# Queries and keys of a head group projected side by side, 512 columns wide

## The chip, the cores and the metric

The kernel runs on one core of a Trainium2 chip. The metric is the device time of one execution in microseconds (us); a result is the median of several runs. The engines are named as in the profile: PE (TensorE, matrix products), PEld (its loads of stationary operands, which overlap with products), DVE (VectorE), ACT (ScalarE), POOL (GpSimd), and SP, whose queue issues most transfers.

## The reference

A trunk of two layers works on 640 tokens: 512 of a new prompt, and 8 running streams with 16 new tokens each. The residual has 1024 features. Each layer is a mixer and a channel mixer, each behind an RMS norm:

```python
# layer 0: gated spatial mixing beside a short gated convolution, then the channel mixer
# layer 1, the mixer that the change is about (for the prompt):
z = x @ w_in                                  # 1024 -> 3072 + 16
q, k, v, f = jnp.split(z, [D_C, 2 * D_C, 3 * D_C], axis=-1)
q = _rmsnorm(q.reshape(b, t, 16, 64), q_norm) # norm over the 64 of a head
k = _rmsnorm(k.reshape(b, t, 16, 64), k_norm)
logf = jax.nn.log_sigmoid(f + b_f)            # "forget values", one a token and head
d = jnp.cumsum(logf, axis=1)
s = einsum('bthd,bshd->bhts', q, k) * 64 ** -0.5 + d_query - d_key
s = where(k_pos <= q_pos, s, NEG_INF)
o = einsum('bhts,bshd->bthd', softmax(s), v)
y = o.reshape(b, t, 1024) @ w_out
# channel mixer, both layers
z = causal_conv3(x @ w_up); y = (silu(gate) * up) @ w_down
```

The streams do the same, each with 256 cached keys and values ahead of its 16 new ones. Outputs are the 640 rows, the new states of the convolutions, and the new keys (behind their norm), values and forget values. All is float32.

## The kernel before

**Arithmetic.** A large product is made of three products of split operands: `weights()` loads a unit of 128 x 1024 float32 weights through SP's queue into `raw`, ACT casts it to `whi` (L88), and DVE subtracts that from `raw` to give the rest, `wlo` (L89). The activations are split likewise into `hh` and `hl`. A product is then hh x whi, hl x whi and hh x wlo. `raw`, `whi` and `wlo` live in the pool `wts` with three buffers each. Products with `whi` or `wlo` take these split operands; transposes, the value products and the streams' products take plain float32.

**Stages.** First mixer, first channel mixer, projections and attention, output projection, second channel mixer. Everything outside the attention has weights stationary and 320 tokens moving (L109), save the first mixer's values (L239: activations stationary, 512 weight columns moving). Engines execute their queues in order. The order of each queue is set when the program is built, by a scheduler that goes by a timeline of its own; buffers of the pools (their `bufs`) limit how far work can run ahead.

**Projections.** The 16 heads are four groups of four. `project(g, ...)` makes queries, keys and values of a group one after the other: for each kind, two units of weights (4 chunks of the features x 256 columns, `io["w_c"]`), and for each of five blocks of 128 tokens 24 matmuls of 256 columns (L507: 8 chunks x 3 products). Two token blocks share a PSUM bank `pj` of 512 columns, of which there are two. ACT evacuates each block into `z` (L510), squares it (L515), DVE sums the squares by head (L516), the root is made by DVE (L151) and POOL (L152), and DVE scales all five blocks by it at once (L519, 1280 elements a partition), for keys once more by the norm's weights (L521). The buffers:

```python
zt = self.zp.tile([P, 5, 256], F32, tag="qk" if kind < 2 else "v", name=k.nm("z"), bufs=3 if kind < 2 else 2)
```

Queries and keys share three such buffers, values have two.

**Forget values.** `decay` is called once, between queries and keys of group 0: 48 matmuls `pf` (L109), a spread of the norm's root over the tokens (matmuls at L174, through `pt`), the logarithm and the running sums `dh`, `dl`, and transfers of these on SP's queue to scratch in HBM (`s_b`, `s_d`, `s_n`; L455 is the first), from which each group reads its rows back (L552 into `kb`; others into `sl` and `sr`).

**Attention.** For each group: transposes (L537) make stacked operands `qa`, `ka`, `qb`, `kb` of two heads (a pair); a prompt block is 128 queries of one head: scores from two matmuls into `sc` (L569, L570), mask (L571), softmax (maximum L589, exponential on ACT L591, reciprocal L592, scaling L594), transposes of the weights `p` into `pt` (L576), a copy `u` (L579 on DVE or ACT), and the value product into `pv` (L583). A pair of streams: `scs` (L634, L641, L644), softmax, transposes (L655), value products (L662), and a transpose back (L666). Within a head pair, which is half a group's attention, eight prompt blocks and two stream pairs follow in a fixed order:

```python
for st in ("b30", "s0", "b31", "o", "b20", "s1", "b21", "b10", "b11", "b00", "b01"):
```

The results are `o[0]` to `o[7]`, two a group. PSUM has two banks for `pj`, two for `sc`, three for `pt`, one for `pv`.

**Filler.** PE needs other work while DVE and ACT do a softmax. This is the next group's projections, and for group 3 the part of the output projection that needs the first three groups only, `po` (L109, also in the `pj` banks):

```python
cut = [6, 6, 6, 6, 6, 4, 4, 4]
for ob in (6, 7, 0, 1, 2, 3, 4, 5):
```

Output blocks 6, 7 and 5 go over four chunks `o[0]` to `o[3]` there, the others over six; the two of group 2 are `o[4]` and `o[5]`. What is left of the output projection comes as blocks `mm` behind the attention.

Of the kernel before, what the change touches and what calls it, by code (L numbers as in the profile page):

```python
# [8 lines left out]
F32 = mybir.dt.float32  # L9
# [34 lines left out]
# columns of the constants of the attention  # L44
# [4 lines left out]
NS = 256 + 16      # keys of a stream  # L49


class Core:
    def __init__(self, ctx, tc, io):
# [38 lines left out]
    def split(self, pool, tags, src):  # L92
        """float32 [128, 640] -> (hi, lo) float32r tiles"""
# [7 lines left out]
    # ---- products, weights stationary, tokens moving  # L101
# [13 lines left out]
    def blocks(self, units, acts, order=None):  # L115
        """one output block for each unit; all share the walk over k, the last chunk closes"""
# [8 lines left out]
    # ---- RMS norm: operands scaled by g now, by the root later  # L125
# [28 lines left out]
    def stats(self, acc, pool, aux):  # L154
        """1/rms for each token, as columns [128, 5]"""
# [8 lines left out]
    def spread(self, rt, pool, aux):  # L164
        """columns [128, 5] -> the same along the free axis of every partition"""
# [45 lines left out]
    # ---- the first mixer  # L211
    def mixer_ab(self, x, load, stats, ring, finish):
        nc, io = self.nc, self.io
        rpool, rtags = ring
        with ExitStack() as es:
            mp = self.pool(es, "ab", bufs=1)
            so = mp.tile([P, 4 * 18], F32, name="sob")
            # v, tokens on partitions
# [24 lines left out]
            # the mask: a query in the first half of a chunk sees no key of the second half  # L243
# [17 lines left out]
            for j in range(4):  # L261
                # gated causal convolution
# [19 lines left out]
            for g in range(4):  # L282
                # spatial gating
# [20 lines left out]
    def project(self, w, acts, order, x, finish, cols=1024, out=None):  # L304
        """x += w^T acts, the first two blocks side by side"""
# [10 lines left out]
    def last_block(self, w, acts, x, out):  # L316
        """the block that ends the program: one half of the tokens leaves while the other is at work"""
# [13 lines left out]
    # ---- the channel mixer  # L331
# [43 lines left out]
class Attention:  # L375
    """forgetting attention of 16 heads: 512 prompt tokens, and 8 streams of 16 behind 256 cached ones"""

    def __init__(self, k, es, rt, o):
# [10 lines left out]
        # sums of the streams as a product over 18 rows: the queries' sums (two parts) against ones,  # L389
        # selectors of (stream, head) against minus the keys' sums (two parts)  # L390
# [22 lines left out]
    def decay(self, h, es):  # L413
        """log forget values and their running sums, heads on partitions"""
# [12 lines left out]
        # log sigmoid(y) = min(y, 0) - log1p(e), e = exp(-|y|)  # L427
# [10 lines left out]
        # running sums, from zero at the start of each stream  # L438
# [25 lines left out]
        # minus the keys' sums, (stream, head) on partitions: cached, then new  # L464
# [12 lines left out]
        # selector rows, the same for each pair of streams  # L477
# [4 lines left out]
        nc.sync.dma_start(out=f(self.sl[2:18]), in_=f(sr))  # L482

    def project(self, g, h, first, after_q=None):
        """q, k, v of four heads, tokens on partitions"""
        k, nc, io = self.k, self.nc, self.io
        z = []
        for kind in range(3):
            if kind == 1 and after_q is not None:
                after_q()  # L490
# [402 lines left out]
```

## Time and profile before

| | |
|---|---|
| median of three runs | 1533.6 us (1533.28 to 1536.43) |
| profiled execution | span 1531.9 us, the only time that the profile gives for it; the median lies 1.7 us above |
| PE, PEld | busy 1517.8 us (99%), 1473.5 us (96%) |
| DVE, ACT, POOL | 59%, 37%, 15% |
| TensorE clock granted | full in all 40 slices of the span |
| HBM | 125.41 MB read, 11.54 MB written: 89 GB/s over the span |
| start of the projections | 679.6 us |
| first attention scores | 738.95 us |
| `po` | from 965.5, to 1030.6 us |
| rest of the output projection from | 1039.1 us |

How to read rows of the trace: a group's row gives line, engine, operation, output <- inputs by the program's names, then partitions x elements, the number of instructions, the busy time in us and the mean of one in ns, and after a second bar the idle time of that engine ahead of them with what ended it. A row of the timeline begins with the start and the duration in us. A row by stretch gives its start and end, its length and the busy time of each engine, with the instructions in brackets. Busy times of PE overlap a little from one instruction to the next, so that the spacing of starts, and not the duration of one, tells what it costs.

### The profile page before, as it was taken

The page shows a single profiled execution, that of the slowest core. Times are in us where ns is not written, and L with a number is a line of the kernel's source. Part 1 is how long each engine was busy: PE and PEld are TensorE (multiplying, and loading weights), DVE is VectorE, ACT ScalarE, POOL GpSimd, SP SyncE. Part 2 cuts the span into 40 slices and gives each one's busy share as a digit, 9 for nine tenths or more (in the row PEclk, how much of TensorE's full clock was granted, in tenths as well). Part 3 has the DMA queues.
Part 4 walks back from the last instruction along what each step waited for, and adds up shares of the span by engine and source line. Part 5 has one row for each costly group of instructions (what it writes and reads, how often), then busy time and mean ns, then how long its engine had stood idle before and what let it go on. Part 6 is the DMA issues. An engine that isn't in the chain of part 4 may idle for free.

```text
span 1531.9 us, 26648 instructions
## 1 busy us (share of the span) xinstructions
PE 1517.8 (99%) x11008; PEld 1473.5 (96%) x11008; DVE 899.1 (59%) x1541; ACT 559.4 (37%) x918; POOL 237.4 (15%) x281
## 2 busy tenths in 40 slices
PE   8999999999999999999999999999999999999999
PEld 6999999999999999999989888888999999999998
DVE  6545437644653655675676766768765466365463
ACT  5422334322322322345545454535432233133231
POOL 5000122201210201143111111003221021021010
PEclk9999999999999999999999999999999999999999
DMA  6222212222223222243544343523222222321313
GB/s 226 77 82 73 77 56 85 68 81 85 62 64 95 64 66 93 62 156 103 180 128 136 122 123 104 183 60 107 83 60 76 87 67 57 98 73 53 107 47 106
DMA packets 52296, 142.90 MB, mean 93 GB/s; under 512 B 6656, under 2 KB 13744, under 8 KB 52048
## 3 DMA queue, kind: packets, MB, share of 16 engines
q1 hardware_dynamic: 45424, 133.79, 28.6%
q10 hardware_dynamic: 6752, 7.41, 1.4%
q8 instruction: 87, 1.43, 0.4%
q14 instruction: 33, 0.27, 0.1%
HBM read 125.41 MB, written 11.54 MB: 89 GB/s over the span
## 4 chain that ended last, share of the span: by engine, by line
PE 96%; DVE 2%; issue 1%; ACT 1%; DMA 0%; POOL 0%; SPq 0%; DVEq 0%; ACTq 0%
PE mm L109 71%; PE pj L507 10%; PE pv L583 3%; PE po L109 2%; PE pt L576 1%; PE mm L239 1%; PE pt L662 1%; PE sc L569 1%; DVE hl L132 1%; PE sc L570 1%; DVE wlo L89 1%; PE scs L641 1%; PE pt L537 1%; PE pt L655 0%; PE scs L634 0%
## 5 line engine op out<-in xcount | busy, mean ns | idle before, releaser
L88 ACT CAST whi<-raw 128x1024 fp32r<-128x1024 f32 (+4 forms) x222 | 207.6, 937 | 494.6 <-PE mm L109 426.1
L109 PE MATMUL mm<-hl,whi 128*128 128x320 f32 x1664 | 379.4, 309 | 0.5 <-DVE hl L132 0.5
L109 PE MATMUL mm<-hh,whi 128*128 128x320 f32 x1664 | 379.8, 309 | 0.0
L109 PE MATMUL mm<-hh,wlo 128*128 128x320 f32 x1664 | 379.2, 309 | 0.0
L109 PEld LDWEIGHTS mm<-hl,whi 128*128 128x128 f32 x1664 | 278.2, 188 | 0.7 <-DVE hl L132 0.7
L109 PEld LDWEIGHTS mm<-hh,whi 128*128 128x128 f32 x1664 | 278.2, 188 | 0.1
L109 PEld LDWEIGHTS mm<-hh,wlo 128*128 128x128 f32 x1664 | 278.0, 188 | 0.0
L89 DVE TENSOR_TENSOR wlo<-raw,whi 128x1024 fp32r<-128x1024 f32 (+4 forms) x222 | 245.5, 1107 | 33.3 <-ACT whi L88 33.0
L109 PE MATMUL mm<-sh,wlo 128*128 128x320 f32 x866 | 197.2, 309 | 1.3 <-DVE wlo L89 1.3
L109 PE MATMUL mm<-sl,whi 128*128 128x320 f32 x866 | 197.2, 309 | 0.0
L109 PE MATMUL mm<-sh,whi 128*128 128x320 f32 x866 | 196.2, 309 | 0.0
L202 POOL COPY so<-zp 128x18 f32<-128x18 f32 x88 | 89.4, 1016 | 570.4 <-DVE zp L191 570.4
L190 DVE TENSOR_TENSOR zp<-mm,rb 128x512 f32<-128x512 f32 x88 | 60.9, 692 | 195.8 <-PE mm L109 195.8
L209 DVE TENSOR_TENSOR x<-mm,x 128x640 f32<-128x640 f32 x79 | 65.0, 823 | 185.6 <-PE mm L109 185.6
L198 DVE SCALAR_TENSOR_TENSOR t<-zp,cst,t 128x656 f32<-128x656 f32 x184 | 165.1, 900 | 10.3 <-ACT t L196 5.6
L109 PEld LDWEIGHTS mm<-sh,wlo 128*128 128x128 f32 x866 | 144.6, 188 | 1.6 <-DVE wlo L89 1.6
L109 PEld LDWEIGHTS mm<-sl,whi 128*128 128x128 f32 x866 | 144.8, 188 | 0.0
L109 PEld LDWEIGHTS mm<-sh,whi 128*128 128x128 f32 x866 | 144.4, 188 | 0.2 <-issue 0.2
L507 PE MATMUL pj<-wlo,hh 128*128 128x256 f32 x480 | 137.7, 287 | 0.7 <-DVE wlo L89 0.7
L507 PE MATMUL pj<-whi,hh 128*128 128x256 f32 x480 | 137.7, 287 | 0.0
L507 PE MATMUL pj<-whi,hl 128*128 128x256 f32 x480 | 137.5, 287 | 0.0
L507 PEld LDWEIGHTS pj<-wlo,hh 128*128 128x128 f32 x480 | 91.6, 191 | 2.8 <-issue 1.6
(188 smaller groups left out, 1691.3 us busy)
## 6 DMA issues: line engine op xcount, KB each, us to landing
raw<-w_up SPq DMA_DIRECT2D x88, 512.0 KB
raw<-w_dn SPq DMA_DIRECT2D x32, 384.0 KB
raw<-w_c SPq DMA_DIRECT2D x24, 512.0 KB
raw<-w_dn SPq DMA_DIRECT2D x32, 320.0 KB
raw<-w_ab SPq DMA_DIRECT2D x16, 512.0 KB
ck<-c_k SPq DMA_DIRECT2D x16, 512.0 KB
cv<-c_v SPq DMA_DIRECT2D x16, 512.0 KB
o_kv<-z ACTq DMA_DIRECT2D x8, 640.0 KB
```

Of the source, the lines that this page charges most:

```text
L88: nc.scalar.copy(out=hi[:, c], in_=raw[:, c])
L89: nc.vector.tensor_tensor(out=lo[:, c], in0=raw[:, c], in1=hi[:, c].bitcast(F32), op=ALU.subtract)
L109: nc.tensor.matmul(outs[h], lhsT=l, rhs=r[:, h * HT:(h + 1) * HT], start=start and k == 0, stop=stop and k == 2)
L132: nc.vector.scalar_tensor_tensor(out=lo, in0=x, scalar=gs, in1=hi.bitcast(F32), op0=ALU.mult, op1=ALU.subtract)
L190: nc.vector.tensor_tensor(out=op, in0=a[:, 0:TP], in1=b[:, 0:TP], op=ALU.mult)
L198: nc.vector.scalar_tensor_tensor(out=cv[:, 0:CW], in0=zp[:, i:i + CW], scalar=w[:, i:i + 1], in1=cv[:, 0:CW], op0=ALU.mult, op1=ALU.add)
L202: self.nc.gpsimd.tensor_copy(out=out.rearrange("p (s c) -> p s c", c=2), in_=zp[:, 496:ZW].rearrange("p (s c) -> p s c", c=18)[:, :, 16:18])
L209: self.nc.vector.tensor_tensor(out=x, in0=ps[:, C0:C0 + T], in1=x, op=ALU.add)
L239: nc.tensor.matmul(pvs[tb], lhsT=l[:, tb * P:(tb + 1) * P], rhs=r[:, (kc % 2) * 512:(kc % 2 + 1) * 512], start=kc == 0 and k == 0, stop=kc ...
L507: nc.tensor.matmul(out[tb], lhsT=l[:, tb * P:(tb + 1) * P], rhs=r[:, c:c + 256], start=kc == 0 and i == 0, stop=kc == 7 and i == 2)
L537: nc.tensor.transpose(t[:, tb * P:(tb + 1) * P], z[i][:, tb, pair * P:(pair + 1) * P], k.ident)
L583: nc.tensor.matmul(ov[64 * hh:64 * hh + 64, i * P:n], lhsT=z[2][:, j, (2 * pair + hh) * 64:(2 * pair + hh) * 64 + 64], rhs=u[:, j * P:(j + ...
```

## The change

`project` becomes `project_qk` and `project_v`, over a common loop `walk`. The weights of a group's queries and keys are laid side by side (`w_qk`: four units of 2 chunks x 512 columns), and a token block takes 24 matmuls of 512 columns and a whole bank. Evacuation (L509 in the changed kernel), squares (L511), sums and roots run over 512 columns; one scaling goes over 2560 elements, and a second over the keys' 1280. Buffers of `z` hold five blocks of 512 columns, two of them; the squares have one buffer. Values are projected as before in two units of 4 chunks x 256 columns, though each token block now has a bank of its own (L528 evacuates it). `decay` is called behind queries and keys of group 0. `wts` has four buffers for `whi` and `wlo`, `raw` keeps three. One argument of the program's set-up is new (`dynamic_dma_scratch_size`). Comments went. The line numbers of what follows shift: L569 and L570 become L575 and L576, L576 becomes L582, L583 L589, L634 L640, L644 L650, L662 L668, L666 L672; the matmul of the projections is L497.

```diff
-        self.wp = pool(ctx, "wts", bufs=3)
+        self.wp = pool(ctx, "wts", bufs=4)
...
-        raw = self.wp.tile([P, 1024], F32, tag="raw", name=self.nm("raw"))
+        raw = self.wp.tile([P, 1024], F32, tag="raw", name=self.nm("raw"), bufs=3)
...
+    def walk(self, us, n, h, pairs, m=512):
+        k, nc = self.k, self.nc
+        out = [None] * 5
+        for tbs in ([(0, 1), (2, 3), (4,)] if pairs else [(tb,) for tb in range(5)]):
+            for tb in tbs:
+                out[tb] = self.pj.tile([P, 512], F32, tag="pj", name=k.nm("pj"))
+            for kc in range(8):
+                wh, wl = us[kc // n]
+                hh, hl = h[kc]
+                c = (kc % n) * m
+                for tb in tbs:
+                    for i, (l, r) in enumerate(((hh, wh), (hl, wh), (hh, wl))):
+                        nc.tensor.matmul(out[tb][:, 0:m], lhsT=l[:, tb * P:(tb + 1) * P], rhs=r[:, c:c + m],
+                                         start=kc == 0 and i == 0, stop=kc == 7 and i == 2)
+            for tb in tbs:
+                yield tb, out[tb][:, 0:m]
+
+    def project_qk(self, g, h):
+        us = [k.weights(io["w_qk"][g, u]) for u in range(4)]
+        zt = self.zp.tile([P, 5, 512], F32, tag="qk", name=k.nm("z"), bufs=2)
+        ss = self.zp.tile([P, 40], F32, tag="ss", name=k.nm("ss"))
+        for tb, o in self.walk(us, 2, h, g == 0):
+            nc.scalar.activation(out=zt[:, tb, :], in_=o, func=AF.Copy, scale=self.rt[:, tb:tb + 1])
+            sq = self.zp.tile([P, 512], F32, tag="sq", name=k.nm("sq"), bufs=1)
+            nc.scalar.activation(out=sq, in_=zt[:, tb, :], func=AF.Square)
+            s = ss[:, tb * 8:tb * 8 + 8]
+            nc.vector.reduce_sum(out=s, in_=sq.rearrange("p (h d) -> p h d", d=64), axis=AX.X)
+            k.rstd_of(s, s, 1.0 / 64)
+        zh = zt.rearrange("p t (h d) -> p (t h) d", d=64)
+        nc.vector.tensor_tensor(out=zh, in0=zh, in1=ss.unsqueeze(2).broadcast_to([P, 40, 64]), op=ALU.mult)
...
+    def project_v(self, g, h):
+        us = [k.weights(io["w_vc"][g, u]) for u in range(2)]
+        zt = self.zp.tile([P, 5, 256], F32, tag="v", name=k.nm("z"), bufs=2)
+        for tb, o in self.walk(us, 4, h, False, 256):
+            nc.scalar.activation(out=zt[:, tb, :], in_=o, func=AF.Copy, scale=self.rt[:, tb:tb + 1])
...
-        z = at.project(g, h, g == 0, decay if g == 0 else None)
+        qk = at.project_qk(g, h)
+        if g == 0:
+            decay()
+        z = qk + (at.project_v(g, h),)
```

The change also moves instructions, since the queues' orders are set anew. Three places:

PE at the first scores of the attention (group 0; `pj` are projections, `sc` prompt scores, `scs` scores of streams). Before, where 37 `pj` of group 1's queries lie ahead of the first score:

```order
L507 MATMUL pj_7604<-whi_7592,hl_6028 128x256
L507 MATMUL pj_7604<-wlo_7593,hh_6027 128x256
L507 MATMUL pj_7604<-whi_7592,hh_6034 128x256
L569 MATMUL sc_7058<-ka_7034,qa_7033 128x512
L634 MATMUL scs_7084<-sr,sl 128x272
L644 MATMUL scs_7084<-kts_7011,qbd_6346 32x16
```

and now, where 70 wide ones of group 1's queries and keys do:

```order
L497 MATMUL pj_7527<-whi_7458,hl_6265 128x512
L497 MATMUL pj_7527<-wlo_7459,hh_6264 128x512
L497 MATMUL pj_7527<-whi_7458,hh_6309 128x512
L575 MATMUL sc_6906<-ka_6882,qa_6881 128x512
L640 MATMUL scs_6932<-sr,sl 128x272
L650 MATMUL scs_6932<-kts_6859,qbd_6346 32x16
L650 MATMUL scs_6932<-kts_6859,qbd_6347 32x16
L576 MATMUL sc_6906<-kb_6884,qb_6883 128x512
```

The two halves of the first score have moved together: before, 31 `pj` matmuls lie between L569 and L570 of this block, now only the streams' products do.

PE where the last projection gives way to the output projection. Before, this is the border of groups 2 and 3 (L576 and L602 are transposes of group 2's last block and of group 3's streams):

```order
L576 MATMUL pt_9715<-cst,p_9708 128x128
L507 MATMUL pj_10074<-whi_10066,hh_6264 128x256
L507 MATMUL pj_10074<-whi_10066,hl_6265 128x256
L507 MATMUL pj_10074<-wlo_10067,hh_6264 128x256
L507 MATMUL pj_10074<-whi_10066,hh_6309 128x256
L507 MATMUL pj_10074<-whi_10066,hl_6310 128x256
L507 MATMUL pj_10074<-wlo_10067,hh_6309 128x256
L602 MATMUL pt_10225<-cst,z_9733 128x128 x2
L602 MATMUL pt_10225<-cst,z_9901 128x128 x2
L109 MATMUL po_10816<-sh_10201,whi_10811 128x320
L109 MATMUL po_10816<-sl_10202,whi_10811 128x320
```

Now the projections end earlier, and 72 `po` matmuls stand within group 2's attention; here is the last of the 72 and what comes after it:

```order
L575 MATMUL sc_8982<-ka_8708,qa_8707 128x128
L576 MATMUL sc_8982<-kb_8710,qb_8709 128x128
L109 MATMUL po_10277<-sh_9605,wlo_10272 128x320
L575 MATMUL sc_8998<-ka_8720,qa_8719 128x128
L576 MATMUL sc_8998<-kb_8722,qb_8721 128x128
L668 MATMUL pt_8901<-cv_8880,up_8905 32x128 x8
L668 MATMUL pt_8901<-z_8548,up_8905 32x128 x4
L582 MATMUL pt_8937<-cst,p_8930 128x128 x3
L672 MATMUL pt_8901<-cst,on_8919 128x128
L582 MATMUL pt_8957<-cst,p_8950 128x128 x2
L589 MATMUL pv_8731<-u_8941,z_8548 64x128 x3
L582 MATMUL pt_8975<-cst,p_8968 128x128 x2
```

From that `po` on, 71 rows of attention follow without a `pj` or `po` between them, until the next `po`, which reads `o[4]`.

DVE in the first mixer (the piece of the difference; L89 splits a weight unit, L151 begins the norm's root, L170 makes the diagonals for its spread):

```order
 L89 TENSOR_TENSOR wlo_429<-raw_427,whi_428 128x1024
+L89 TENSOR_TENSOR wlo_486<-raw_484,whi_485 128x1024
 L151 TENSOR_SCALAR rt_270<-aux_264 128x5
 L170 TENSOR_SCALAR t_274<-cst,rt_270 128x128 x5
-L89 TENSOR_TENSOR wlo_486<-raw_484,whi_485 128x1024
 L89 TENSOR_TENSOR wlo_551<-raw_549,whi_550 128x1024
```

One split has moved from behind the root and its diagonals to ahead of them.

More of the change, by code (lines that the diff above doesn't have):

```diff
@@ new lines, in project_qk @@
+    def project_qk(self, g, h):
+        k, nc, io = self.k, self.nc, self.io
+        us = [k.weights(io["w_qk"][g, u]) for u in range(4)]
[10 more added lines that the diff above has]
+        nc.vector.tensor_tensor(out=zh, in0=zh, in1=ss.unsqueeze(2).broadcast_to([P, 40, 64]), op=ALU.mult)
+        zk = zt[:, :, 256:512].rearrange("p t (h d) -> p t h d", d=64)
+        nc.vector.tensor_tensor(out=zk, in0=zk, in1=self.cst[:, O_KN:O_KN + 64].unsqueeze(1).unsqueeze(1).broadcast_to([P, 5, 4, 64]), op=ALU.mult)
+        nc.scalar.dma_start(out=io["o_kv"][0, :, :, 256 * g:256 * g + 256].rearrange("t p c -> p t c"), in_=zt[:, :, 256:512])
+        return zt[:, :, 0:256], zt[:, :, 256:512]
@@ L830, in _layout @@
     wc = a["w_in_c"][0]
-    d["w_c"] = con(wc[:, :3072].reshape(2, 4, P, 3, 4, 256).transpose(4, 3, 0, 2, 1, 5)).reshape(4, 3, 2, P, 1024)
+    rows = lambda w, n: con(w.reshape(8 // n, n, P, 1024 // n).transpose(0, 2, 1, 3)).reshape(8 // n, P, 1024)
+    grp = lambda kind, g: wc[:, 1024 * kind + 256 * g:1024 * kind + 256 * g + 256]
+    d["w_qk"] = np.stack([rows(np.concatenate([grp(0, g), grp(1, g)], 1), 2) for g in range(4)])
+    d["w_vc"] = np.stack([rows(grp(2, g), 4) for g in range(4)])
     wf = np.zeros((1024, P), f)
```

44 lines of the change are left out of this document (4 added, 40 removed).

## The prediction

> **What bounds the kernel now.** I read the page first (busy shares, clock, the chain that ended last), then the chain in order of time, the time by stretch, and PE's waits.
>
> ```profile
> span 1531.9 us, 26648 instructions
> PE 1517.8 (99%) x11008; PEld 1473.5 (96%) x11008; DVE 899.1 (59%) x1541; ACT 559.4 (37%) x918; POOL 237.4 (15%) x281
> PEclk9999999999999999999999999999999999999999
> PE 96%; DVE 2%; issue 1%; ACT 1%; DMA 0%; POOL 0%; SPq 0%; DVEq 0%; ACTq 0%
> PE mm L109 71%; PE pj L507 10%; PE pv L583 3%; PE po L109 2%; PE pt L576 1%; PE mm L239 1%; PE pt L662 1%; PE sc L569 1%; DVE hl L132 1%; PE sc L570 1%; DVE wlo L89 1%; PE scs L641 1%; PE pt L537 1%; PE pt L655 0%; PE scs L634 0%
> ```
>
> TensorE is the bound: 96% of the chain is its work, at the full granted clock, and the projections that the change rewrites (`pj`, L507) are 10% of it. So the question is what an instruction costs PE, and where PE waits. By stretch (first mixer's start; projections and decay of group 0; attention filled with `pj`; attention filled with `po`; the last attention rows alone; after it), the columns being length, then the busy time of PE, PEld, DVE, ACT, POOL, the clock, DMA share and GB/s:
>
> ```profile
> 20.00:40.00 20.00, 20.00 (x100) 16.98 (x99) 10.28 (x13) 5.19 (x7) 8.86 (x8) 1.00 0.39 123
> 679.60:738.90 59.30, 58.58 (x480) 58.38 (x479) 35.54 (x60) 30.64 (x54) 17.16 (x23) 1.00 0.40 124
> 738.90:965.70 226.80, 226.80 (x2090) 200.29 (x2090) 153.88 (x448) 110.31 (x284) 30.31 (x30) 1.00 0.39 126
> 965.70:1030.60 64.90, 64.90 (x533) 56.26 (x531) 46.64 (x127) 27.39 (x71) 0.27 (x4) 1.00 0.42 130
> 1030.60:1039.10 8.50, 7.90 (x75) 5.82 (x74) 6.39 (x25) 3.72 (x13) 0.00 (x0) 1.00 0.09 33
> 1039.10:1076.20 37.10, 35.35 (x243) 34.75 (x243) 28.13 (x31) 18.69 (x28) 15.12 (x12) 1.00 0.34 110
> ```
>
> PE never rests while projections fill behind the attention. It rests a little (8.50 less 7.90, so 0.6 us) in the only stretch of attention without any filler, at the end.
>
> **Width: 480 pairs of 256 columns become 480 of 512.** The pieces of the chain give the spacing of matmuls that follow each other:
>
> ```profile
> 31.74 2.72 PE mm L239 x12
> 149.72 70.55 PE mm L109 x481
> 890.67 6.82 PE pj L507 x57
> ```
>
> That is 226.7 ns for 512 columns (2.72/12), 146.7 for 320 and 119.6 for 256. From 256 to 320 columns the step is 27.1 ns for 64, from 320 to 512 it is 80.0 for 192: 0.42 ns a column both times, so each instruction carries about 13 ns that don't depend on its width. Two of 256 take 239.2, one of 512 takes 226.7: 12.5 ns saved. The 512 row has the same form as the new one (activations stationary, weights moving). Queries and keys were 2 x 120 matmuls a group and become 120, over 4 groups 480 fewer: 480 x 12.5 = **-6.0 us**, all on the path. The bounds are 0 (were the 13 ns a matter of columns) and -6.4 (13.3 ns, from the 320 row).
>
> The Trainium skill has a rule that speaks against this: in "TensorE: Matmul & The Clock Gate", section "Back-to-back issue gap", it gives a warm spacing of columns over 2.4 GHz plus about 2.5 ns. By it a pair would save 2.6 ns and the whole 1.2 us, an estimate from that page. The rows above disagree with it, with 119.6 ns where it has 109.2.
>
> **Switches: fewer returns to projections.** A projection matmul that follows a transpose or a value product costs more:
>
> ```profile
> 763.95 0.66 PE L537 MATMUL pt<-cst,z 128*128 128x128 f32 x4
> 764.36 0.36 PE L507 MATMUL pj<-whi,hh 128*128 128x256 f32 x1
> 764.56 0.28 PE L507 MATMUL pj<-whi,hl 128*128 128x256 f32 x1
> 764.68 0.28 PE L507 MATMUL pj<-wlo,hh 128*128 128x256 f32 x1
> ```
>
> Behind the return the second matmul starts 0.20 us after the first, the third 0.12 after that: 0.08 us lost. In the order of the built program PE goes 136 times from plain float32 work (transposes, products with `pv`) back to split operands, in the changed order 109 times: 27 x 0.08 = **-2.2 us**, between 0 (if the loss falls on another instruction) and -4.6 (if as much is lost on the way in).
>
> **Filler: it is used up earlier.** Attention of one half-group takes PE 16.7 us by itself: the stretch 738.90 to 965.70 holds 3 x 351 `pj` matmuls, at 0.120 us 126.4 of its 226.8, and 100.4 is left for six halves.
>
> ```profile
> L507 PE MATMUL pj<-wlo,hh 128*128 128x256 f32 x351 | 101.3, 289 | 0.0
> L109 PE MATMUL po<-sh,wlo 128*128 128x320 f32 x84 | 23.7, 313 | 0.0
> ```
>
> In the order before, the last projection stands beside the last row of group 2's attention, and all 3 x 84 = 252 `po` matmuls fill behind group 3. In the order after, projections run ahead (a whole group's queries and keys have two buffers, where three half-size ones held them back), 72 `po` matmuls are spent inside group 2, and then the next needs o[4], which is complete only with group 2's last stream. Counted from the order with the durations before, three stretches have no filler: about 13 us at the end of group 1 (values of group 3 wait for a buffer that group 1 reads), 20.6 in group 2's second half, and 14 at the end of group 3, where before had 8.5. Together 47.6 instead of 8.5 us. What idle time do they hold? The last stretch before has 0.6 in 8.5, 7%: 47.6 x 0.07 - 0.6 = +2.8 us. The other bound is VectorE. Its softmax rows of one half-group, the eighth part of sums like these,
>
> ```profile
> L571 DVE TENSOR_TENSOR sc<-sc,mskb 128x128 f32<-128x128 f32 x64 | 18.6, 296 | 28.4 <-PE sc L570 28.2
> L592 DVE RECIPROCAL l<-l 128x1 f32<-128x1 f32 x80 | 12.8, 160 | 8.1 <-ACT p L591 6.7 <-ACT pp L591 0.7
> L589 DVE TENSOR_REDUCE m<-sc 128x1 f32<-128x512 f32 x16 | 11.0, 687 | 0.2
> L579 DVE COPY u<-pt 128x512 f32<-128x512 f32 x16 | 11.0, 687 | 4.6 <-PE pt L576 4.6
> L594 DVE TENSOR_SCALAR p<-p,l 128x512 f32<-128x512 f32 x16 | 7.8, 485 | 0.4
> ```
>
> add up, over all 18 groups from L571 to L670, to 137.7/8 = 17.2 us, hardly more than PE's 16.7. Were VectorE held to the 75% that it reached in the last stretch (6.39 of 8.50), a half would take 22.9 us and not 16.7, and 47.6 us of PE work would hold 17.7 us of idle time: +17 us. I take **+4 us**, near the row that measured such a stretch, since the two score buffers keep two blocks under way; a little above it because the stretches are longer and hold the 512-wide blocks.
>
> **The decay behind keys, not queries.** The forget values now come after queries and keys, not between them: group 0's 120 wide matmuls take 27.2 us (120 x 0.2267), then 48 `pf` 7.1 (48 x 0.1467), where 96 `pj`, `pf` and 24 `pj` stood. `pf` then ends near 716, not 702.3, and the first scores near 749:
>
> ```profile
> 702.34 1.27 PE L174 MATMUL pt<-t,ones 128*128 128x128 f32 x10
> 738.95 0.40 PE L569 MATMUL sc<-ka,qa 128*128 128x512 f32 x1
> 744.04 0.39 PE L570 MATMUL sc<-kb,qb 68*128 68x512 f32 x1
> 717.96 0.73 ACT L446 CAST dh<-t 16x640 fp32r<-16x640 f32 x1 [0.59 <-DVE t L443]
> 718.71 0.34 SPq L455 DMA_DIRECT2D s_b<-dh  x1
> 736.26 1.60 SPq L552 DMA_DIRECT2D kb<-s_b  x1
> ```
>
> From the end of `pf` to L570, which needs the sums read back by SP, there were 41.7 us and now are some 34. The chain needs 15.6 to `dh` and, on SP's queue, 12 to 17 more to the `kb` rows, so 28 to 33 with a landing of 2 or 3: **+0.7 us**, between 0 and +6. The move past SP's queue itself is free: `w_f` is loaded two units later, 24 loads of 512 KB stay 24. PE is covered meanwhile by values of group 0 (14.4 us) and queries and keys of group 1.
>
> **The fourth split-weight buffer.** It lets VectorE split one unit earlier everywhere. Two of PE's waits on a split could go:
>
> ```profile
> PE mm L239 <- DVE wlo L89: 1.6, 1, 1.6
> PE mm L109 <- DVE wlo L89: 1.3, 1, 1.3
> ```
>
> The first is of the start, where the load is late and not the buffer, so at most the second: **-0.7 us**, between 0 and -1.3. On the other side a split now stands ahead of the first mixer's root on VectorE's queue:
>
> ```profile
> 28.70 0.17 DVE L151 TENSOR_SCALAR rt<-aux 128x5 f32<-128x5 f32 x1 [0.88 <-PE aux L159]
> 30.17 1.07 DVE L170 TENSOR_SCALAR t<-cst,rt 128x128 f32<-128x128 f32 x5 [1.30 <-POOL rt L152]
> 34.76 1.05 PE L174 MATMUL aux<-t,ones 128*128 128x128 f32 x8
> ```
>
> Behind the waiting split stand the root, POOL's power and the diagonal, for which PE's L174 waits. They ended at 31.24, 3.5 us early. The split's load cannot start before its buffer is free near 24.8; with cast and split it may end near 32: **+0.3 us**, 0 to +1.
>
> **Costed at nothing.** Evacuations (60 of 256 columns become 20 of 512 and 20 of 256), squares and sums (40 each become 20) and scalings (12 become 8) lie on ACT and VectorE, which have 51% and 32% free while PE works:
>
> ```profile
> L510 ACT ACTIVATE z<-pj,rt 128x256 f32<-128x256 f32 x60 | 25.6, 471 | 29.7 <-PE pj L507 26.6 <-DVE t L436 2.9
> L519 DVE TENSOR_TENSOR z<-z,ss 128x1280 f32<-128x1280 f32 x8 | 11.9, 1490 | 1.9 <-POOL ss L152 1.6
> ```
>
> The 2560-element scaling holds VectorE some 3.0 us in one piece (twice 1.49), so a split or a softmax step behind it may come 1.5 late: 0 to +1. Values now fill a bank in 24 x 0.12 = 2.9 us, not 5.8, with two banks: if ACT's 0.47 us stands behind a full queue, PE waits, 0 to +2. If that cover is gone, the next late thing is the bank.
>
> **Sum** against the profiled span: 1531.9 - 6.0 - 2.2 + 4 + 0.7 - 0.7 + 0.3 = 1528.0. The runs' median of 1533.6 lies 1.7 above that span, so the forecast is **1529.7 us**. Two in a thousand, 3.1 us, is about what a measurement here tells from no change.
>
> **The rivals.**
> - The unfilled stretches cost 5 to 11 us, a share of 12 to 24% idle: for it speaks that PE is in order and a late softmax step stops everything behind it; against it the 7% above. About 1533, no change. Chance 0.24.
> - VectorE becomes the bound in those stretches: +17 in place of +4, 1542.7, slower. It decides from an idle share of 26%, 11.1 us. For it: 17.2 against 16.7 us a half; against it: queues of two engines overlap, and VectorE sheds its splits there. Chance 0.10.
> - The change doesn't do what it says: the 13 ns grow with the columns, and the wide matmuls take 239. Then 1529.7 + 6.0 = 1535.7, no change. The 226.7 row speaks against it. By the skill's rule above the saving would be 1.2 us and the time 1534.5; the trace agrees with it only in that 512 is cheaper than twice 256. Chance 0.05.
> - The sums come late: 5 us of wait at L570's place, 1534.7; chance 0.05, of which 0.02 slower.
>
> The forecast itself has 0.56 and runs from 1524.5 to 1530.5. Faster 0.56; within 0.2% 0.24 + 0.05 + 0.03 = 0.32; slower 0.12. The range, 1524.5 to 1537, takes in every case but VectorE's and the best bounds (0.05 below).
>
> **What would show it.** `pj` pieces of 227 ns a matmul; fewer `pj` pieces; PE idle time of a few us between 900 and 980 and in the last 14 us before the blocks `mm` of the output projection; the second score product (L576 in the changed kernel) without a wait near 749; no wait of PE on `wlo` after 1039. The forecast is wrong if PE's idle time in the unfilled stretches passes 8 us, or if PE waits for evacuated banks inside the values.

## The result, and the profile after

The changed kernel takes 1543.8 us (median of five runs, 1539.2 to 1544.2); the kernel before took 1535.4 us in five runs beside it. The ratio is 1.0053, with an interval of 1.0040 to 1.0067: slower by half a per cent, where 1529.7 us and faster was forecast. The range ended at 1537. The profiled execution has a span of 1541.7 us, 9.8 more than that of before.

The page of the changed kernel (span; busy time by engine; granted clock in 40 slices; the chain by engine and by line):

```profile
span 1541.7 us, 25569 instructions
PE 1517.5 (98%) x10528; PEld 1448.5 (94%) x10528; DVE 894.5 (58%) x1497; ACT 556.4 (36%) x878; POOL 230.8 (15%) x261
PEclk9999999999999999999999999999999999999999
PE 95%; DVE 2%; ACT 1%; DMA 1%; issue 1%; SPq 0%; DVEq 0%; ACTq 0%
```

PE is busy for the same 1517.5 us, although 480 matmuls are gone and the work is less. The page's slices of 39 us show a clock of nine tenths or more throughout, and hide what follows. The time by stretch splits the program in three (before the projections; projections and attention; after the attention). Before the change:

```profile
0.00:679.78 679.78, 672.47 (x4520) 666.71 (x4521) 376.70 (x504) 230.25 (x311) 112.37 (x129) 1.00 0.29 87
679.78:1039.08 359.30, 357.98 (x3170) 320.54 (x3168) 242.45 (x658) 172.02 (x418) 47.56 (x57) 1.00 0.39 124
1039.08:1531.92 492.84, 487.34 (x3321) 486.21 (x3320) 279.91 (x379) 157.13 (x190) 77.49 (x96) 1.00 0.27 79
```

And after it:

```profile
0.00:681.55 681.55, 673.64 (x4520) 667.29 (x4521) 379.47 (x505) 231.31 (x312) 110.61 (x129) 1.00 0.28 88
681.55:1049.70 368.15, 356.81 (x2691) 295.02 (x2689) 236.20 (x614) 168.07 (x378) 43.14 (x37) 0.99 0.38 120
1049.70:1541.65 491.95, 487.09 (x3321) 486.22 (x3320) 278.81 (x378) 157.02 (x189) 77.04 (x96) 1.00 0.26 79
```

The start is 1.8 us longer, the attention with its projections 8.85, the end 0.9 shorter. In the attention PE now idles 368.15 less 356.81, so 11.3 us, where it idled 1.3; and the clock there is 0.99 and not 1.00. Finer stretches of the changed kernel show where:

```profile
905.00:921.00 16.00, 14.82 (x154) 11.40 (x153) 12.47 (x43) 5.75 (x19) 0.00 (x0) 1.00 0.43 146
921.00:928.00 7.00, 4.83 (x27) 4.59 (x28) 2.79 (x4) 4.71 (x11) 0.00 (x0) 0.76 0.33 76
955.00:982.00 27.00, 24.94 (x249) 17.96 (x249) 20.95 (x75) 12.81 (x39) 0.00 (x0) 1.00 0.38 125
982.00:992.00 10.00, 6.97 (x36) 4.75 (x35) 6.24 (x11) 5.30 (x11) 0.00 (x0) 0.66 0.48 140
1040.00:1049.70 9.70, 7.56 (x77) 5.62 (x75) 7.46 (x33) 4.50 (x16) 0.00 (x0) 1.00 0.01 3
```

Those are the end of group 1, the border to group 2, group 2's second half, the border to group 3, and the end. Nearly half of the idle time (2.2 and 3.0 us) stands at the two borders, and there the clock falls as well. The waits of PE name what ended last:

```profile
PE po L109 <- ACT sh L97: 3.0, 1, 3.0
PE mm L239 <- DVE wlo L89: 2.5, 1, 2.5
PE pj L497 <- ACT z L528: 2.2, 1, 2.2
PE pv L589 <- DVE u L585: 1.9, 2, 1.1
```

The third of these stands at group 2's border. There, in order of time, the work of ACT:

```profile
920.65 0.68 ACT L550 ACTIVATE qa<-pt,qn 64x512 fp32r<-64x512 f32 x1 [0.55 <-PE pt L543]
921.24 0.57 ACT L567 COPY x<-pv 128x512 f32<-128x512 f32 x1
921.70 1.49 ACT L615 ACTIVATE qbd<-pt,qn 64x128 f32<-64x128 f32 x4
923.20 0.84 ACT L528 ACTIVATE z<-pj,rt 128x256 f32<-128x256 f32 x2
```

And PE's in the same place, five of its rows:

```profile
920.91 0.65 PE L543 MATMUL pt<-cst,z 128*128 128x128 f32 x4
923.73 0.58 PE L497 MATMUL pj<-whi,hh 128*128 128x256 f32 x1 [2.17 <-ACT z L528]
924.11 0.41 PE L497 MATMUL pj<-whi,hl 128*128 128x256 f32 x1
924.32 0.41 PE L497 MATMUL pj<-wlo,hh 128*128 128x256 f32 x1
927.29 0.28 PE L497 MATMUL pj<-wlo,hh 128*128 128x256 f32 x1
```

Group 3's values wait for a bank; the bank waits for its evacuation; and that stands in ACT's queue behind an operand, the copy of the group's output and four scaled copies of the streams' queries, 1.49 us. When PE gets on, its matmuls of 256 columns stand 0.21 us apart (924.11, 924.32) until about 927, and 0.12 after that: the clock is granted at half for 3.4 us. At group 3's border it is the split of o[4] (L97) that stands behind the same ACT instructions:

```profile
981.51 0.68 ACT L550 ACTIVATE qa<-pt,qn 64x512 fp32r<-64x512 f32 x1 [0.55 <-PE pt L543]
982.10 0.56 ACT L567 COPY x<-pv 128x512 f32<-128x512 f32 x1
982.56 1.49 ACT L615 ACTIVATE qbd<-pt,qn 64x128 f32<-64x128 f32 x4
984.07 0.58 ACT L553 CAST ka<-pt 64x512 fp32r<-64x512 f32 x1
984.67 0.72 ACT L97 CAST sh<-x 128x640 fp32r<-128x640 f32 x1
```

PE waits 3.0 us, and half clock follows for 6.8 us.

So the attention's length is split below into idle time of PE, time lost to the lower clock (each slice of 1 us times one less the clock granted in it), and the rest, which is called the work.

| profiled execution | attention, us | idle | lost to clock | work |
|---|---|---|---|---|
| before | 359.3 | 1.3 | 0 | 358.0 |
| changed | 368.1 | 11.3 | 5.1 | 351.7 |

The change bought 6.3 us of PE's work and gave back 10.0 in idle time and 5.1 in clock.

### The profile page after: what moved, and what is told of

Read it like the earlier page. It is cut to its first block, busy times and chain, and to the rows that moved or that the text cites. A ratio compares the mean times of both kernels' runs of the same rounds, so it can differ in the third digit from the quotient of the medians.

```text
span 1541.7 us, 25569 instructions
## 1 busy us (share of the span) xinstructions
PE 1517.5 (98%) x10528; PEld 1448.5 (94%) x10528; DVE 894.5 (58%) x1497; ACT 556.4 (36%) x878; POOL 230.8 (15%) x261
## 4 chain that ended last, share of the span: by engine, by line
PE 95%; DVE 2%; ACT 1%; DMA 1%; issue 1%; SPq 0%; DVEq 0%; ACTq 0%
PE mm L109 71%; PE pj L497 10%; PE po L109 3%; PE pv L589 2%; PE mm L239 1%; PE pt L582 1%; PE pt L668 1%; PE sc L575 1%; PE sc L576 1%; PE scs L647 1%; DVE wlo L89 1%; DVE hl L132 0%; PE pf L109 0%; PE pt L661 0%; PE pt L543 0%
## 5 line engine op out<-in xcount | busy, mean ns | idle before, releaser
L89 DVE TENSOR_TENSOR wlo<-raw,whi 128x1024 fp32r<-128x1024 f32 (+4 forms) x222 | 245.9, 1110 | 27.8 <-ACT whi L88 27.1
L497 PE MATMUL pj<-whi,hh 128*128 128x512 f32 (+1 forms) x320 | 110.8, 346 | 2.3 <-ACT z L528 2.2
L497 PE MATMUL pj<-whi,hl 128*128 128x512 f32 (+1 forms) x320 | 109.3, 342 | 0.0
L497 PE MATMUL pj<-wlo,hh 128*128 128x512 f32 (+1 forms) x320 | 108.7, 341 | 0.0
L196 ACT ACTIVATE t<-zp,cst 128x656 f32<-128x656 f32 x92 | 77.6, 846 | 36.6 <-DVE zp L191 36.6
```

What stands on the lines that cost most here:

```text
L89: nc.vector.tensor_tensor(out=lo[:, c], in0=raw[:, c], in1=hi[:, c].bitcast(F32), op=ALU.subtract)
L196: nc.scalar.activation(out=cv[:, 0:CW], in_=zp[:, 2:ZW], func=AF.Copy, scale=w[:, 2:3])
L497: nc.tensor.matmul(out[tb][:, 0:m], lhsT=l[:, tb * P:(tb + 1) * P], rhs=r[:, c:c + m], start=kc == 0 and i == 0, stop=kc == 7 and i == 2)
```

## The experiments

All are edits of the changed kernel, except for the last two. The times are medians, the ratios are against the kernel before. That took 1534.2 to 1534.5 us beside these runs and 1535.4 beside the changed kernel, so by the ratios the gains on the changed kernel are about 1 us smaller than by the medians (e4: 6.8 and not 7.9; e5: 5.4 and not 6.5). Each attention is split as above, in one profiled execution.

| run | us | ratio | attention | idle | clock | work |
|---|---|---|---|---|---|---|
| e1 one buffer for queries and keys | 1546.9 | 1.0077 (1.0062 to 1.0093) | 371.3 | 15.4 | 6.8 | 349.0 |
| e2 scaling by block | 1539.5 | 1.0028 (1.0018 to 1.0037) | 364.3 | 8.6 | 3.4 | 352.3 |
| e3 cut at four | 1542.5 | 1.0052 (1.0035 to 1.0069) | 364.8 | 12.1 | 10.2 | 342.4 |
| e4 streams' queries on VectorE | 1535.9 | 1.0009 (0.9999 to 1.0019) | 361.4 | 8.3 | 1.7 | 351.4 |
| e5 forget values first | 1537.3 | 1.0018 (1.0009 to 1.0027) | 361.3 | 9.3 | 3.4 | 348.6 |
| e6 narrow again | 1543.8 | 1.0064 (1.0051 to 1.0078) | 370.1 | 6.7 | 3.4 | 360.0 |
| e7 = e2 + e4 + e5 | 1535.6 | 1.0007 (0.9998 to 1.0015) | 359.7 | 6.5 | 1.7 | 351.6 |
| e8 = e7 + copies on ACT | 1532.8 | 0.9991 (0.9982 to 1.0000) | 357.9 | 5.8 | 0 | 352.1 |
| e9 = e8, forget values after two blocks | 1533.8 | 0.9994 (0.9985 to 1.0003) | 359.5 | 6.2 | 1.7 | 351.7 |
| e10 = e9, last streams early | 1534.4 | 1.0000 (0.9991 to 1.0009) | 358.4 | 7.1 | 0 | 351.3 |
| e11 old kernel, two moves | 1536.5 | 1.0015 (1.0007 to 1.0024) | 359.6 | 3.0 | 0 | 356.7 |
| e12 old kernel, four buffers | 1535.2 | 1.0003 (0.9995 to 1.0012) | 360.7 | 1.7 | 0 | 359.0 |

**e4: shorten the two waits.** The four copies at L615 go from ACT to VectorE.

```diff
-                nc.scalar.activation(out=qbd..., in_=tr..., func=AF.Copy, scale=self.qn[a])
+                nc.vector.tensor_scalar(out=qbd..., in0=tr..., scalar1=self.qn[a], scalar2=None, op0=ALU.mult)
```

> The changed kernel with the four scaled copies of the streams' queries (L615) made by VectorE in place of ACT at each group's start; ACT takes 1.49 us for them there while PE waits for what stands behind them in ACT's queue. Theory A: both long waits get shorter by about 1.5 us (2.2 to 0.7, 3.0 to 1.5), stay under 2 us, and the clock is not halved behind them (-1.7 and -3): -5 to -8, 1536 to 1539 us. If the clock is halved by something else than the length of the wait, it drops at the same two places and the time is 1540 to 1542.

Its waits of PE at the two borders:

```profile
PE po L109 <- ACT sh L97: 1.4, 1, 1.4
PE pj L497 <- ACT z L528: 0.7, 1, 0.7
```

And the stretches around the borders to group 2 and to group 3:

```profile
917.00:928.00 11.00, 10.34 (x84) 8.47 (x85) 5.96 (x16) 6.36 (x15) 0.00 (x0) 1.00 0.37 98
974.00:984.00 10.00, 8.37 (x54) 6.32 (x52) 8.53 (x17) 5.49 (x11) 0.00 (x0) 0.83 0.58 177
```

The waits are 0.7 and 1.4 us, as expected; the clock no longer falls at the first, and falls for 3.4 us at the second, though its wait is under 2 us. 7.9 us came off, a little better than forecast (1535.9): 3.0 of idle time and 3.4 of clock in the attention, the rest at the start and in spread. Sixteen small copies of 0.37 us on the wrong engine were, in this arrangement, worth most of the loss.

**e1: let the filler last.**

```diff
-        zt = self.zp.tile([P, 5, 512], F32, tag="qk", name=k.nm("z"), bufs=2)
+        zt = self.zp.tile([P, 5, 512], F32, tag="qk", name=k.nm("z"), bufs=1)
```

> The changed kernel with one buffer for queries and keys in place of two, so that the next group's can only be evacuated once the present group's last operands are transposed; two of five token blocks can wait in PSUM. In the built order the filler then lasts through every half-group, as before the change. Theory A (the loss is PE's waiting where attention has no filler, with a halved clock behind each wait of more than about 2 us; the wide products themselves gained what was forecast): the waits of 2.2 us on ACT at group 2's start and of 3.0 us at group 3's go, with the half-clock matmuls behind them; the attention takes 350 to 354 us in place of 368.2, and the time is 1525 to 1531 us. Theory B (the wide evacuations, squares and the scaling of 2560 elements hold ACT and VectorE up wherever they stand, so PE waits anyway): the time stays at 1538 or above. Theory C (the loss is mostly of the start, 1.8 us in the profile): at most 8 us come from the attention and L239 still ends near 40.8.

A miss: 1546.9, slower still. Its waits of PE in the attention, the longest first:

```profile
PE sc L575 <- ACT p L597: 5.8, 3, 1.9
PE pj L497 <- ACT z L509: 2.8, 3, 0.9
PE sc L575 <- DMA qa<-qa: 2.6, 1, 2.6
```

The waits at the borders of theory A did go. But now groups 0, 1 and 2 begin without filler, and there PE waits 1.9 us each time: both score buffers are taken until the first softmax has read one. How much work is unfilled tells little; the start of a group is where PE needs cover most, since no other block is under way yet. Theory B gave the time but isn't borne out, as the longest waits are the softmax's, with ACT idle for 3.7 to 3.8 us ahead of its exponential (it waits for VectorE's maximum), and the evacuations' are 2.8 us in all, in three.

**e2: the long scaling in pieces.**

```diff
-        nc.vector.tensor_tensor(out=zh, in0=zh, in1=ss.unsqueeze(2).broadcast_to([P, 40, 64]), op=ALU.mult)
-        nc.vector.tensor_tensor(out=zk, in0=zk, ...)            # keys, 1280 elements
+        for tb in range(5):
+            zh = zt[:, tb, :].rearrange("p (h d) -> p h d", d=64)
+            nc.vector.tensor_tensor(out=zh, in0=zh, in1=ss[:, 8 * tb:8 * tb + 8]..., op=ALU.mult)
+            nc.vector.tensor_tensor(out=zh[:, 4:8], in0=zh[:, 4:8], ..., op=ALU.mult)
```

> The changed kernel with the scalings of queries and keys made for each token block (ten instructions of 512 and 256 elements a group in place of two of 2560 and 1280). In the built order the filler of group 1 lasts to its end; the stretch without filler in group 2's second half stays, and that at the end. Theory A: the 2.2 us wait at group 2's start and its 3.4 us of half clock go (about -4), the rest stays: 1538 to 1541 us. Theory B (the long scaling on VectorE is itself what PE waits for): the other stretches shrink too, 1530 to 1535 us.

1539.5, in A's range: idle time falls by 2.7 us and the clock's loss by 1.7. The wait at group 2's border is still there with 1.8 us, so it was not the mechanism that A named; what shrank is the stretch ahead of it, where filler now lasts (to 915, not 909). The 1.7 us of clock came off at the other border, behind a wait of 3.0 us as before, so they can't be credited to the edit.

**e3: more filler without o[4].**

```diff
-    cut = [6, 6, 6, 6, 6, 4, 4, 4]
+    cut = [4, 4, 4, 4, 4, 4, 4, 4]
```

> The changed kernel with only the first four chunks of each output block put behind the attention (192 po matmuls in place of 252, none of which needs o[4]); the other four chunks follow after the attention, 60 matmuls more there (8.8 us moved, not added). Filler then lasts through group 2, and about 22 us at the end have none. Theory A: the 3.0 us wait for the split of o[4] at group 3's start goes with the half clock behind it (-6) and 20 us of unfilled attention in group 2 (-4); the last stretch grows by 14 us (+3): 1536 to 1540 us, and no clock below full between 970 and 1000. If instead VectorE sets the pace in any unfilled stretch (PE busy 75%), the time in the last 22 us is some 29 us and the gain is gone: 1541 to 1545.

The time is 1542.5, within the second case. The wait on o[4] is gone, but its place is taken at the end: 8.8 us of the attention's work were moved behind it, and 10.2 us went to the clock, most of it after 1000, where group 3 had run out of filler. The filler ended at 996.5, so that 48 us had none where 22 were expected; PE was busy for 87% of them, where the second case had 75%, in part at half clock; so the time fits that case, and its cause does not. (The profiled execution is the slowest of its five, 1547.5.)

**e5: forget values first.** The late running sums had cost no wait of their own. The first scores of the changed kernel:

```profile
750.42 0.40 PE L575 MATMUL sc<-ka,qa 128*128 128x512 f32 x1
750.74 0.39 PE L640 MATMUL scs<-sr,sl 18*128 18x272 f32 x1
```

They come at 750.4, 11.5 us later than before, right behind other work. But that work is projections of group 1. By the built orders 190 wide and 120 narrow matmuls precede the first score, 57.5 us, where 397 narrow ones, 47.6 us, did: 10 us of filler spent as cover.

```diff
-        qk = at.project_qk(g, h)
         if g == 0:
             decay()
+        qk = at.project_qk(g, h)
```

> The changed kernel with the forget values made first, ahead of group 0's queries and keys. In the built order 160 wide matmuls and not 190 then stand ahead of the first score, so 7 us of filler (30 x 0.227) are left for later. Theory A (the late running sums cost no wait, but the projections that covered them were the filler missing at the end): stretches without filler shrink by some 7 us, idle time of PE in the attention falls from 11.3 to 6 to 9 us and at least one half-clock period goes: from the first of pf and pj to the output projection's rest 360 to 364 us in place of 368.1, 1536 to 1540 us. Rival (the place of the decay is worth nothing, since the same matmuls are done in any order): 1541 to 1544.

1537.3: 6.5 us came back, in A's range. In the profiled execution 2.1 are of idle time and 1.7 of clock: the wait at group 2's border is 0.7 us, with no half clock behind it. Another 3.1 are in what is called the work here, for which no cause is shown, and 1.6 were lost at the start, where PE now waits 1.0 us ahead of `pf`.

**e6: narrow again.** The projections of groups 1 to 3 make two passes over the chunks.

```diff
-            for kc in range(8):
+            e = m if pairs else 256
+            for j, kc in [(j, kc) for j in range(0, m, e) for kc in range(8)]:
...
-                c = (kc % n) * m
+                c = (kc % n) * m + j
...
-                        nc.tensor.matmul(out[tb][:, 0:m], ..., rhs=r[:, c:c + m],
+                        nc.tensor.matmul(out[tb][:, j:j + e], ..., rhs=r[:, c:c + e],
```

> The changed kernel with the projections of queries and keys of groups 1 to 3 in matmuls of 256 columns again (two passes over the eight chunks into the halves of the same bank; group 0 stays wide). If a wide matmul saves 12.5 ns against two narrow ones, 360 of them add 4.5 us of PE work; as filler lasts 4.5 us longer, idle time falls by part of that: 1541 to 1546 us, with idle time of PE in the attention of 7 to 10 us in place of 11.3. If the wide form saves nothing (rival: the 13 ns grow with the columns), the work stays as it is and the time is 1537 to 1541.

The time is the same as with the wide ones, 1543.8 (the intervals of the two ratios overlap), but it is made up otherwise:

```profile
679.42:1049.54 370.12, 363.45 (x3050) 316.83 (x3048) 237.94 (x614) 168.91 (x378) 41.27 (x37) 0.99 0.38 120
```

The work is 8.3 us more, idle time and clock 6.4 less. By the built orders PE goes back 121 times from plain float32 to split operands in the attention, and 97 times in the changed kernel (124 in the kernel before): 360 x 12.5 ns = 4.5 us would be of the width, 24 x 0.08 = 1.9 of the returns, and 1.9 are left over. So the wide form is cheaper, and in this arrangement worth nothing: what it saves is filler.

**e7, e8: the edits together.** e7 has the edits of e2, e4 and e5. e8 adds:

```diff
-        if i % 2:
-            nc.vector.tensor_copy(out=u, in_=t[:, 0:n])
-        else:
-            nc.scalar.copy(out=u, in_=t[:, 0:n])
+        nc.scalar.copy(out=u, in_=t[:, 0:n])
```

> The changed kernel with three edits together: forget values first, the streams' queries scaled by VectorE, scalings by token block. Theory A: the waits at group borders stay under 1.5 us, so at most one half-clock period; idle time of PE in the attention 4 to 7 us; 1529 to 1533 us, 2 to 5 below the kernel before. If the three edits mend the same loss, no better than the single best of them: 1534 to 1537.

> As the run with three edits, and all copies u of transposed weights on ACT, which takes from VectorE the 16 of 512 and 16 of 256 elements, some 14 us over the attention. Theory A (in the stretches without filler the chain of softmax steps sets the pace, and VectorE, busy 75 to 80% there, is the fuller engine): those stretches get 5 to 10% shorter, 1 to 3 us: 1527 to 1531 us. If ACT's queue is what delays (its copy stands behind exponentials and weight casts): the same or up to 3 us slower.

e7 came out at 1535.6, no better than e4 alone: the three edits mend one loss. e8 gained 2.7 us more, but missed its range (1527 to 1531). The attention of e7, then of e8:

```profile
680.50:1040.23 359.73, 353.26 (x2688) 292.16 (x2688) 245.21 (x661) 161.80 (x361) 43.13 (x36) 1.00 0.38 122
680.63:1038.53 357.90, 352.08 (x2689) 290.54 (x2689) 229.95 (x629) 173.07 (x393) 41.93 (x36) 1.00 0.39 123
```

With 15 us less on VectorE (245.2 to 230.0) the attention is 1.8 us shorter. Of that 1.7 are the half clock that e7 has behind a wait of 1.4 us on the split of o[4], and e8, with the same wait, has not; 0.7 are idle time, and the work is 0.5 more. This is the fastest version, 1532.8, but within 0.2% of the kernel before.

**e9, e10: two more waits.** In e9 the forget values come after the first two token blocks (a hook in the loop over blocks, and a split buffer of their own for `w_f`); in e10 group 2's last stream pairs go first (`("s0", "b30", "s1", "b31", ...)`) with the split of o[4] behind them, and group 3's projections and the splits of o[0] to o[3] are called ahead of them.

> The run with four edits, but the forget values made between the first two token blocks of group 0's queries and keys and the rest (with a split-weight buffer of their own, since all four are held by the queries' and keys' units). The same 160 wide matmuls stand ahead of the first score. In the run before it PE waited 1.0 us ahead of pf for the last residual add of the stage before and 1.7 us ahead of the third token block for a bank; pf now covers the second, and pj of the other pool begins the stage. Theory A (each of these waits was on the path): 2 to 2.7 us less, 1529.5 to 1531 us. Rival (the running sums 10 us later make PE wait at the first scores): no gain, 1532 to 1535.

> As the run just above, and both stream pairs of group 2's second half moved to its front, with the split of o[4] put right behind them, so that the output projection can go on a little before group 2 ends (in the built order the stretch without filler there moves by some blocks but hardly shrinks, 12.8 in place of 13.4 us of work). Theory A: the 1.4 us wait on ACT's split goes, 1 us or so: 1528 to 1530.5. Rival (the first blocks of a half-group need the filler more than the last ones): no gain or a loss of up to 2 us.

Neither gained. In e9 the wait ahead of pf went, while that for a bank grew from 1.7 to 2.1 us, and had half clock behind it in the profiled execution; in e10 the wait on the split of o[4] is 1.4 us as before. Both outcomes are the rivals' of the two expectations.

**e11, e12: parts on the old kernel.** e11 has the moves of e4 and e8 there; e12 the fourth buffer for `whi` and `wlo`.

> The kernel before the change with the two moves between engines alone: the streams' queries scaled by VectorE, all copies u by ACT. Theory A (the moves mend waits that the change brought; before it PE idled 1.3 us in the attention): 1532.5 to 1534.5 us, 0 to 1 below before. Rival (VectorE's pace cost the old kernel too, within PE's small gaps): 1529 to 1531.5, and then the wide projections themselves have bought nothing.

> The kernel before the change with four buffers for whi and wlo (and the program's set-up argument) alone. If the fourth buffer is what shortened the part after the attention from 492.8 to 491.95 us, it is 491.8 to 492.1 here and PE no longer waits for wlo there, and the time 0.9 lower, 1533.5 us. If the fourth buffer is to blame for the longer wait in the first mixer, L239 ends at 40 to 41 us and not at 39; if that is chance, it may end at either.

e11 is slower than before by 0.15%, outside both ranges given for it, so the moves mend what the change brought, and bring nothing without it: PE waits 1.9 us there for a bank that VectorE empties. e12 takes the time of the kernel before (ratio 1.0003), where 0.9 us less was expected. e12's stretches, up to the projections and after the attention:

```profile
0.00:682.00 682.00, 673.65 (x4520) 667.33 (x4521) 379.44 (x505) 231.29 (x312) 110.58 (x129) 1.00 0.29 88
1042.68:1534.64 491.96, 487.11 (x3321) 486.23 (x3320) 278.90 (x378) 156.93 (x189) 77.02 (x96) 1.00 0.26 79
```

The end is 491.96 with the fourth buffer, 492.84 and 492.88 without (before, e11): 0.9 us are the buffer's. The attention is 1.4 us longer than before, in another order on PE (six more returns, by the built orders). The start is 682.0 here and 679.3 to 681.6 in other kernels that begin this stage with the same projections. PE's wait on `wlo` there is 1.4 to 2.5 us from one execution to the next, and in four of the twelve profiles with four buffers (those with a wait of 2.5 us) half clock stood behind it, in neither of the two with three (1.6 and 1.1 us). That is too few to blame the buffer.

## Why the prediction was wrong

- **Filler, the step that failed: the borders between groups were put at nothing.** +4 stood for 47.6 us without filler, and +17 as the end of its range. The attention idled 10.0 us more and lost another 5.1 to the clock, 15 in all. In the stretches themselves the price was near. Here they are in the changed kernel, the first two up to the border:

```profile
909.40:921.50 12.10, 10.92 (x97) 8.20 (x95) 8.69 (x37) 5.89 (x19) 0.00 (x0) 1.00 0.52 180
956.80:978.70 21.90, 19.84 (x214) 13.80 (x212) 19.48 (x72) 11.48 (x36) 0.00 (x0) 1.00 0.42 138
1034.60:1049.70 15.10, 12.96 (x144) 9.56 (x142) 11.67 (x44) 5.92 (x20) 0.27 (x4) 1.00 0.07 20
```

  They hold 43.7 us of work and 5.4 of idle time, 11% and not 7%; less the 0.6 of before that is +4.8. What stood at nothing are the waits of PE at the two borders, 2.2 and 3.0 us, and the half clock behind them, 1.7 and 3.4. The row of 8.50 us was the *end* of a half-group, without borders; at a border ACT's queue holds 2.5 to 3.2 us of operand work, and a filler matmul whose bank or operand ACT must provide waits behind it. e4 shows this by experiment: with 1.5 us less in that queue the two waits are 0.7 and 1.4 us. ACT's share of busy time (51% free) said nothing of that queue. And the two score buffers don't keep two blocks under way at a group's start, where no softmax is done yet; that shows in e1 only.
- **Clock, a term that wasn't there.** A wait costs again what the half clock takes behind it: 5.1 us in the attention.
- **Decay, +0.7.** No wait, as forecast, and first scores at 750.4 where 749 was said. But "PE is covered meanwhile" priced the cover at nothing, while the projections that covered were used up: 10 us of filler. e5 leaves 7 us of it (30 wide matmuls) for later and takes 6.5 us less.
- **Values' banks, 0 to +2.** The wait is 2.2 us (0.7 in e4), just past the end of that range, and the half clock behind it was not in it. The prediction had named this and more than 8 us of idle time in the unfilled stretches as signs that it would be wrong; both came (with the border waits they hold 10.6).
- **Scaling in one piece, 0 to +1.** 4.3 us, by way of the filler (e2).
- **Width, -6.0, and switches, -2.2: right in kind.** Pieces of the chain:

```profile
681.71 7.28 PE pj L497 x32
718.68 5.76 PE pj L497 x48
```

  They give 227.5 ns (wide) and 120 (values). Returns fell by 27 as counted. The work fell by 6.3, not 8.2; that is the width's 6.0 almost alone, and no run shows by itself what the returns gave.
- **Fourth buffer, -0.7.** 0.9 (e12, behind the attention). At the first mixer's root, where +0.3 stood, PE waited for nothing. The start's 1.8 us had no term: the split that PE waits for came at 18.2 us and not 18.1, but PE had been there 0.7 us earlier and so waited 2.5 us and not 1.6, and half clock followed (1.7 us).
- **The cause given for the running ahead was wrong.** The prediction said that three half-size buffers held the projections back. The kernel before, built with four of them, has the same order on PE, so they didn't; what did stays open. In the changed kernel the two buffers do allow it: with one (e1) the last projection comes at 977 and not 936.
- **The rivals.** That of VectorE came nearest in time (1542.7), by luck: PE idled 11% in the unfilled stretches and not 26%, and the long waits at the borders were ACT's. There is something in it for the middle stretch above, where VectorE was busy for 19.5 of 21.9 us; with less of its work (e8) PE's idle time there fell from 2.1 to 0.7 us. The rival of 5 to 11 us had the idle time right (10.0) with another cause, a late softmax, and no clock; hence its 1533.

Sum by what was measured, on the profiled spans: work -6.3, idle +10.0, clock +5.1, start +1.8, end -0.9: +9.7, where the spans differ by 9.8.

## What to carry to other kernels

Work that fills another stage's gaps is a stock: count where it is spent, and what is left for the last gap, before making it cheaper, moving it ahead or giving it to a late chain as cover. A wait that was covered is not free when the cover runs out elsewhere. At the borders between groups read the queue of the engine that frees the banks, instruction by instruction; its share of busy time over the stage hides it.

## What the runs showed of the hardware

The granted clock of TensorE fell to 0.50 up to 2.5 us after waits of PE of 1.4 to 3.0 us, and stayed there for 3 to 10 us, with matmuls of 256 columns 0.21 us apart and not 0.12. Every loss in the tables is a multiple of 1.7 us, that is, of 3.4 us at half clock. It fell after every wait of 2.2 us or more within the program, and after some of the shorter ones: after 1.4 us in e4 and not in e8, after 1.9 once in e1 (at 912) and once in e3, and not at another place of e1 (832) nor in e11, not after 1.63 in the kernel before, after 2.1 in e9 and not in e10, and twice behind short ones in a row (0.5 and 0.7 us in e6; 0.7, 0.5 and 0.5 in e3). The Trainium skill ("TensorE: Matmul & The Clock Gate", section "What's actually happening") has half rate after an idle window of about 3.4 us that runs freely; the half rate and the chance in it agree, but shorter waits sufficed here. The program's first matmuls stand at that rate too, 0.43 us apart for 512 columns and not 0.23, until 10.5 us in the kernel before and 8.6 in the changed one, though the view's clock says 1.00 there. Times within one kernel go with the clock: e4's ten runs reach from 1533.2 us at a mean clock of 1.000 to 1539.3 at 0.996.
